# A hybrid attention layer on one core: other K tiles for VectorE's row products, and four kinds of small steps in other places

## The chip, the core and the metric

The kernel runs on one core of a Trainium2 chip. The metric is the device time of one execution in microseconds (us). The core has five engines with an instruction queue each, run in order: TensorE (PE, matrix products; its weight loads are shown as PEld), VectorE (DVE), ScalarE (ACT), GpSimd (POOL) and SyncE (SP), which here issues nearly all loads from main memory. An instruction waits on semaphores for what it needs; while it waits, all behind it on the same engine waits too.

## What is computed

One layer over 256 latent tokens (D = 2048) with a context prefix of 256 tokens, all in float32. Modulation rows come from a conditioning vector and one large matrix (adaLN). The modulated tokens go through one input projection whose columns feed a bidirectional gated linear attention (GLA, 8 heads, with decay factors) and a differential attention (8 heads). Both branches are projected, merged by sigmoid gates, projected again and added to x; then a gated MLP with a width-3 convolution follows. Cut to what matters:

```python
sh1, sc1, g1, sh2, sc2, g2 = split(silu(c) @ w_ada + b_ada, 6)       # w_ada: 2048 x 12288
sh1c, sc1c, ... = split(silu(c_ctx) @ w_ada + b_ada, 6)
h_l, h_c = modulate(rms_norm(x), sh1, sc1), modulate(rms_norm(ctx), sh1c, sc1c)
gq, gk, gv, gr, gaf, gab, dq, dk, dv = split(h @ w_in)               # for h_l and h_c
# GLA, per chunk, forwards and backwards, b = cumsum of log decays:
o_inter = (qc * exp(b)) @ state
o_intra = sum_d qc kc exp(b_i - b_j) @ vc                            # lower triangle
state = exp(b_last) * state + (kc * exp(b_last - b)).T @ vc
o_diff = (softmax(q1 k1) - lam * softmax(q2 k2)) @ v
g_a, g_b = split(sigmoid(h_l @ w_gate + b_gate))
x = x + g1 * (g_a * (ya @ w_proj_gla) + g_b * (yb @ w_proj_diff)) @ w_out
x = x + g2 * (conv_ffn(modulate(rms_norm(x), sh2, sc2)))             # w_up, conv, silu(gate) * val, w_down
```

## The kernel before

**Weights.** Every weight arrives from main memory as 128 x 1024 floats (512 KB) in a buffer "wraw", of which there are four (`fetch`, L231). `split` (L207) makes two halves of it: the upper, whi, is a rounding copy by ScalarE (L212), the lower, wlo, is the difference raw − whi by VectorE (L219). There are three buffers of each. PE then makes three products per piece: upper weight by upper and by lower activation, lower weight by upper activation. A PE wait for wlo means that VectorE came late with that difference.

**First stage** (L384 to about L690). All steps are pinned in program order. For each of the 16 K tiles (128 rows of D) the shift and scale of the modulation are needed before the tile can be swept. For 13 tiles PE computes them: `ada_rows` makes the products "ab" (16 in the code, 32 instructions in the profile) out of four 512 KB quarters of the adaLN matrix ("ada", `load_ada`), then two transposes (L537). They stand inside the sweep of the K tile before. For the three tiles in DOT_TILES, VectorE computes them instead: the matrix lies transposed in "w_ad1t", `load_halves` loads four 512 KB halves of it per tile, and `run_dots` (L426) makes eight row products (a product summed along the row, 128 x 1024) for two streams. The list DOTS says how many of the row products come at each K step, and each half is loaded in the step before its first row product. `dotted` gathers the sums on GpSimd. Then `stage` modulates the tile of each stream (L553, then ScalarE's rounding, L555, then the lower half, L559), and PE sweeps the tile with one piece of `w_in` ("sweep", loaded by `load_sweep`, 448 KB). Loads of the stage go to SP's queue in program order, and "ada" has SLOTS = 10 buffers for quarters and halves together.

**The rest of the adaLN rows.** The other 64 rows of 128 adaLN columns are computed by VectorE alone, as 128 row products "araw" of 128 x 1024 (L379), spread over all later stages to fill VectorE's free time. `ada_load` (L370) loads 512 KB into one of two buffers, `ada_dot` (L377) makes the row product and puts the sum into ada2; it may not come ahead of the last wlo on VectorE (copied[1]). `ada_next(n)` paces both: it adds n to what is due, and each unit due is one product and one load of a later one. With two buffers the load for one product cannot be issued before the product two places ahead of it has ended.

**GLA stage.** The value columns come in chunks (`gv_chunk`, "gvb"), and four pairs of heads (`gla_pair`, L813 on) run beside them under a higher priority. Each pair makes decay sums bfb (cumulative log decays) and rc by scans on VectorE, then rc and qe, exponents by ScalarE times keys and queries by VectorE (L853 and L862), then the scores. The scores are made in groups (RUNS): a whole product, a product of the two chunks (`factors(None)`), and seven levels of the triangle. Each level needs a difference "away" by GpSimd (L930), exponents by ScalarE (L933) and a product e by VectorE (L935). After the first group of scores the decayed keys rc are transposed (`turned_keys`, L867); the states are made with them, and qe is used at the end of the pair.

**Differential stage.** `dv_chunk(0)` (L1051 on) sums four banks over eight pieces of the value weights, each piece split as above, and leaves them to `emptied` (L1054), in which ScalarE copies banks 0 and 2 and VectorE banks 1 and 3 (L1055). Then come query tiles 0 to 3 (`dq_tile`), `dv_chunk(1)`, and the eight heads. `dq_tile` sums one tile of 16 K products from two pieces, adds the two half banks (nraw, L290), squares them and makes head norms with a sum on PE (hss). Each head's attend and scores have a higher priority. Beside the heads run the gate tiles (`gate_tile`, 32 of them, three per head and the rest behind), and query tiles 4 to 7. dv_chunk, dq_tile and gate_tile each call ada_next, gate_tile with an entry of GATE_ADA.

**Tail.** The last stage, "down" (L1419), sums 44 K tiles for each half of the columns. Behind its last pieces come the y steps: `added_rows` (L1428) multiplies a bank by the gate (L1432) and adds the residual row (L1433).

**What sets the order.** Outside the first stage a scheduler places each instruction on its engine's queue by priorities and by its own time estimates, and by the `after` ties written in the code. So instructions may stand in another order than they are written.

Of the kernel before, what the change touches and what calls it, by code (L numbers as in the profile page):

```python
# [13 lines left out]
AF = mybir.ActivationFunctionType  # L14
ALU = mybir.AluOpType
# [3 lines left out]
P = 128  # L19
D = 2048  # L20
T = 256
# [19 lines left out]
UPS = 6  # L41
CONVS = 7
SLOTS = 10
DOT_TILES = 7, 11, 15
DOTS = [0, 0, 2, 2, 2, 2, 1, 2, 2, 3, 1, 2, 2, 3]
LATE_ADA = {13: 1, 14: 2}
ROWS_AT = [4, 3, 2, 1]
WARM = 14
GATE_ADA = [0.25] * 12 + [0.5] * 4 + [0.75] * 8 + [1] * 6 + [0] * 2
NRM = [(0, 0)] * 2 + [(j, j + 1) for j in range(12)] + [(12, 14), (14, 16)]  # L50

_VEC = {}
# [100 lines left out]
def layer_kernel(tc, I, out):  # L153
    nc = tc.nc
    V, S, G, PE = nc.vector, nc.scalar, nc.gpsimd, nc.tensor
    es = ExitStack()
    with es:
# [40 lines left out]
        copied = [None, None]  # L198
# [187 lines left out]
        with tc.tile_pool(name="first", bufs=1) as p1:  # L386
# [21 lines left out]
            cbc = p1.tile([P, D], F32, name="cbc")  # L408
            junk = hp.tile([P, 1024], F32, tag=f"x{KT - 1}", name="junk")
            sums2 = p1.tile([P, len(DOT_TILES), 2, 2, 2], F32, name="sums2")  # L410
            dots = [(0, *d) for d in ((0, 0, 0), (0, 1, 0), (0, 0, 1), (1, 0, 0), (1, 0, 1), (0, 1, 1), (1, 1, 0), (1, 1, 1))]
            dots += [(n, u, q, t) for n in range(1, len(DOT_TILES)) for u in (0, 1) for q in (0, 1) for t in (0, 1)]
            dots_of, at = [], 0
            for n in DOTS + [0] * KT:
                dots_of.append(dots[at:at + n])
# [313 lines left out]
        def ada_next(n):  # L729

            ada_due[0] += n
            while ada_at[0] < min(128, int(ada_due[0])):
                if len(ada_raw) == ada_pool[1]:
                    ada_dot()
                ada_load()
# [16 lines left out]
        with tc.tile_pool(name="gla", bufs=1) as pg:  # L752
# [5 lines left out]
            qk = {}  # L758
# [54 lines left out]
            def gla_pair(p):  # L813
# [35 lines left out]
                        V.tensor_tensor_scan(rc[:, 1, 1:], onec[:, :T - 1], m[:, T:2 * T - 1],  # L849
                                             0.0, op0=ALU.mult, op1=ALU.add)  # L850

                S.activation(rc, rc, AF.Exp, scale=1.0 / 16)
                V.tensor_tensor(rc, rc, qk[p][:, 2:3, :].to_broadcast([P, 2, T]), op=ALU.mult)  # L853
                bl = pg.tile([P, 4], F32, tag="bl", name="bl")
                V.tensor_scalar(bl[:, 0:1], bfb[:, 0, P - 1:P], 1.0 / 16, None, op0=ALU.mult)
                V.tensor_scalar(bl[:, 1:2], bfb[:, 1, P:P + 1], 1.0 / 16, None, op0=ALU.mult)
                qe = pg.tile([P, 2, T], F32, tag="qe", name="qe")
                S.activation(qe[:, 0, :P], bfb[:, 0, :P], AF.Exp, scale=1.0 / 16)
                S.activation(qe[:, 0, P:], bfb[:, 0, P:], AF.Exp, scale=1.0 / 16, bias=bl[:, 0:1])
                S.activation(qe[:, 1, :P], bfb[:, 1, :P], AF.Exp, scale=1.0 / 16, bias=bl[:, 1:2])  # L860
                S.activation(qe[:, 1, P:], bfb[:, 1, P:], AF.Exp, scale=1.0 / 16)
                V.tensor_tensor(qe, qe, qk[p][:, 0:1, :].to_broadcast([P, 2, T]), op=ALU.mult)  # L862

                at = pg.tile([P, 2, 2, T], F32, tag="at", name="at")

# [1 line left out]
                def turned_keys():  # L867

                    b = aux_bank("kT")
                    kn = pg.tile([P, 512], F32, tag="l", name="kn").rearrange("p (a b c) -> p a b c", a=2, b=2)  # L870
                    for d in range(2):
                        for c in range(2):
                            PE.transpose(b[:, (2 * d + c) * P:(2 * d + c + 1) * P], rc[:, d, c * P:(c + 1) * P], ident)
                    return kn, S.copy(kn.rearrange("p a b c -> p (a b c)"), b)
# [42 lines left out]
                def factors(li):  # L917

                    e = pg.tile([P, 2, T], F32, tag="e", bufs=3, name="e")
                    if li is None:  # L920
                        S.activation(e[:, 0, P:], bfb[:, 0, P:], AF.Exp, scale=1.0 / 16)
                        S.activation(e[:, 0, :P], bfb[:, 1, :P], AF.Exp, scale=1.0 / 16)
                        S.activation(e[:, 1, :P], bfb[:, 0, :P], AF.Exp, scale=-1.0 / 16, bias=bl[:, 0:1])
                        S.activation(e[:, 1, P:], bfb[:, 1, P:], AF.Exp, scale=-1.0 / 16, bias=bl[:, 1:2])
                    else:
                        m = LEVELS[li]
                        g = T // (2 * m)
                        away = pg.tile([P, 512], F32, tag="m", name="away")
                        mids = shifted[:, :, m - 1:T:2 * m].unsqueeze(3).to_broadcast([P, 2, g, 2 * m])
                        G.tensor_tensor(away.rearrange("p (a g n) -> p a g n", a=2, g=g),  # L930
                                        bfb.rearrange("p a (g n) -> p a g n", g=g), mids, op=ALU.subtract)
                        for i, (first, step, o, back, sign) in enumerate(((m, T - m, m, -m, 1), (0, T + m, 0, m, -1))):
                            S.activation(view(e[:, i, :], o, [back, 2], [2 * m, g], [1, m]),  # L933
                                         view(away, first, [step, 2], [2 * m, g], [1, m]), AF.Exp, scale=sign / 16)
                    V.tensor_tensor(e, e, qk[p][:, 0:2, :], op=ALU.mult)  # L935
                    return e


# [9 lines left out]
                for n, levels in enumerate(RUNS):  # L948
                    group = ([] if n else whole) + [level(li) for li in levels]
                    if n == 1:  # L950
                        kept = pg.tile([P, 2, T], F32, tag="e", bufs=3, name="e")
                        state = kept[:, 0, :].rearrange("p (a b) -> p a b", a=2)
                        scored(group[::-1], states, [emptied])
                    else:
                        scored(group[::-1])
                    if n == 0:
                        kn, emptied = turned_keys()

                obs = [aux_bank("o", j) for j in range(2)]
# [79 lines left out]
        with tc.tile_pool(name="diff", bufs=1) as pd:  # L1039
# [11 lines left out]
            def dv_chunk(j):  # L1051
                banks = [acc_bank("dvb") for _ in range(4)]

                def emptied(t):  # L1054
                    (V.tensor_copy if t % 2 else S.copy)(dv[:, t, 512 * j:512 * (j + 1)], banks[t])  # L1055


                turn = [6, 7, 0, 1, 2, 3, 4, 5] if j else list(range(8))
                for q in turn:
                    if q in turn[1:3]:  # L1060
                        flush(latest)
                        flush()
                    raw = fetch(I["w_dv"][j, q].rearrange("p a b -> p (a b)"), 1024)
                    both = split(raw, 1024)
                    ws = []
                    for a in range(2):
                        def halves_of(a=a):
                            if j or q > 1:
                                ada_next(0.875 if j else 1)
                            return [w[:, a * 512:(a + 1) * 512] for w in both]  # L1070
                        ws.append((2 * q + a, halves_of))
                    value_rows(banks, ws, 512, 2 * turn[0], 2 * turn[-1] + 1, emptied)
                    if not j and q >= 4:
                        after(V.tensor_tensor(oy[q - 4], oy[q - 4], gr[q - 4], op=ALU.mult), copied[1])
                    if j:
                        nc.gpsimd.dma_start(X4[2 * q][:, 2:, :], A[2 * q + 1])
                        A[2 * q + 1] = X4[2 * q][:, 2:, :]

            def dq_tile(h):
                dq[h] = pd.tile([P, T], F32, tag="dq", bufs=4, name="dq")  # L1080
                b = aux_bank("dq") if h < 2 else acc_bank("dq")
                if h < 2:
                    ada_next(1)
                col_tile(I["w_in"][15 - NGK + h], A, b)
                heads_norm(b, nwt[:, 1:2], lambda o: roped(tp, dq[h], o),
                           *[t[:, h % 2 * T:(h % 2 + 1) * T] for t in nts[:2]], lambda: nts[2][:, h % 2 * T:(h % 2 + 1) * T])
# [90 lines left out]
            for h in range(HEADS):  # L1177
                with tc.high_priority(500):
                    normed_head, emptied = attend(h)
                    if h + 1 < HEADS:  # L1180
                        halves(h + 1)
                        scores(h + 1, emptied)
                    normed_head()
                if h < 4:
                    dq_tile(4 + h)
                for _ in range(3):
                    gate_tile(order.pop(0))
            while order:
# [134 lines left out]
        with tc.tile_pool(name="ffn", bufs=1) as pf:  # L1323
# [101 lines left out]
            def place(at):  # L1425
                return shared(8 + 2 * (at // 2), at % 2, "y")

            def added_rows(h, t, n):  # L1428

                o = slice(1024 * h + 512 * n, 1024 * h + 512 * (n + 1))  # L1430
                y = place(4 * h + 2 * t + n)
                V.tensor_tensor(y, banks[h][t][n], cb[:, o], op=ALU.mult)  # L1432
                V.tensor_tensor(y, y, rows[2 * h + n][t], op=ALU.add)  # L1433
                return y

# [16 lines left out]
                    residual(h, k)  # L1452

            ws = [pieces(k) for k in range(last, FT)]
            y, late = added_rows(1, 1, 1), place(0)
            for n in range(2):
                for t in range(2 - n):
                    for k in range(last, FT):
# [26 lines left out]
```

## Time and profile before

| what | value |
|---|---|
| median of 3 runs | 1657.08 us (1656.51 to 1658.12) |
| the profiled execution | 1658.09 us |
| its span, first to last instruction | 1656.3 us |
| granted TensorE clock | 1.000 |
| ScalarE busy | 904.2 us (55%) |
| GpSimd busy | 289.1 us (17%) |
| bytes moved | 372.75 MB, mean 225 GB/s |
| row products araw, 128 | 161.1 us busy, 1263 ns each |
| wlo by VectorE, 466 | 564.5 us busy, 1212 ns each |

Times in the profile are those of one profiled execution, counted in microseconds from the start of its span, and the rows name an engine, the line of the kernel, the operation and output<-input by the program's names. A timeline row is start, duration, engine, line, operation, shape, number of instructions in the row (x), and in brackets the idle time of the engine just ahead of it and what ended that. "SPq" is a load issued by SP. PE's matmuls overlap a little, so that the step from one start to the next tells more than the durations.

### The profile page before, as it was taken

What the parts mean: (1) busy time and instruction counts of PE and PEld (TensorE: products, weight loads), DVE (VectorE), ACT (ScalarE), POOL (GpSimd) and SP (SyncE); (2) the same over time, 40 slices, a digit from 0 to 9 for tenths busy, and PEclk for the clock granted to TensorE, in tenths of its full rate; (3) what the DMA queues carried; (4) which work ended last, traced back from release to release, by engine and by line L of the source; (5) the groups of instructions that cost most, each with busy time, mean ns of one, the idle gap of its engine ahead of it and who ended that gap; (6) DMA issues with size and microseconds to landing.
All of it is one profiled execution on the core that took longest, in us unless ns stands there. A gap on an engine that the chain in (4) does not pass through costs nothing.

```text
span 1656.3 us, 25739 instructions
## 1 busy us (share of the span) xinstructions
PE 1645.7 (99%) x9509; PEld 1407.3 (85%) x9509; DVE 1303.5 (79%) x2031; ACT 904.2 (55%) x1503; POOL 289.1 (17%) x328
## 2 busy tenths in 40 slices
PE   9999999999999999999999999999999999999998
PEld 7679988888887888888888988888888888888887
DVE  5787888797679888888988887888888888745544
ACT  5235466674346767656645675555555555433332
POOL 0001221230011000001114101122212212684000
PEclk9999999999999999999999999999999999999999
DMA  9996744345785556687887566777777776777764
GB/s 382 408 370 221 237 144 155 117 138 184 248 270 186 176 182 202 228 272 256 265 284 218 181 196 225 233 225 239 241 231 238 225 237 211 210 218 204 221 196 130
DMA packets 111966, 372.75 MB, mean 225 GB/s; under 512 B 14560, under 2 KB 19680, under 8 KB 111840
## 3 DMA queue, kind: packets, MB, share of 16 engines
q1 hardware_dynamic: 102112, 362.51, 66.6%
q0 software_dynamic: 5696, 4.24, 1.0%
q10 hardware_dynamic: 4032, 4.37, 0.8%
q8 instruction: 74, 1.21, 0.3%
q14 instruction: 52, 0.43, 0.1%
HBM read 364.73 MB, written 2.10 MB: 221 GB/s over the span
## 4 chain that ended last, share of the span: by engine, by line
PE 92%; DMA 4%; DVE 3%; issue 1%; ACT 0%; SPq 0%; DVEq 0%
PE down L1419 14%; PE upg L282 9%; PE upv L282 9%; PE gate L282 7%; PE upv L284 5%; PE upg L284 5%; PE sweep L391 4%; PE gate L284 4%; PE mix L282 4%; DMA araw<-in_w_ada 2%; PE mix L284 2%; PE gr L282 2%; PE pga L282 2%; PE pgb L282 2%; PE dk L355 2%; PE dk L356 2%
## 5 line engine op out<-in xcount | busy, mean ns | idle before, releaser
L212 ACT CAST whi<-wraw 128x1024 fp32r<-128x1024 f32 (+3 forms) x502 | 516.1, 1029 | 491.9 <-PE down L1419 138.6
L219 DVE TENSOR_TENSOR wlo<-wraw,whi 128x1024 fp32r<-128x1024 f32 (+3 forms) x466 | 564.5, 1212 | 219.3 <-ACT whi L212 216.8
L282 PE MATMUL upg<-x,whi 128*128 128x512 f32 x656 | 229.0, 391 | 0.0
L282 PE MATMUL upv<-x,whi 128*128 128x512 f32 x656 | 229.0, 391 | 0.0
L1419 PE MATMUL down<-whi,g 128*128 128x512 f32 x698 | 215.0, 389 | 0.0
L284 PE MATMUL upv<-x,wlo 128*128 128x256 f32 x656 | 182.8, 280 | 0.0
L284 PE MATMUL upg<-x,wlo 128*128 128x256 f32 x656 | 182.6, 280 | 0.0
L379 DVE CUSTOM_DVE_ANT_0 araw<-araw,cb 128x1024 f32<-128x1024 f32 x128 | 161.1, 1263 | 24.0 <-DMA araw<-in_w_ada 23.8
L282 PE MATMUL gate<-x,whi 128*128 128x512 f32 x512 | 179.5, 396 | 0.0
L219 POOL TENSOR_TENSOR wlo<-wraw,whi 128x1024 fp32r<-128x1024 f32 x36 | 86.9, 2415 | 395.3 <-ACT whi L212 395.3
L1419 PEld LDWEIGHTS down<-whi,g 128*128 128x128 f32 x698 | 130.9, 188 | 27.2
L282 PEld LDWEIGHTS upg<-x,whi 128*128 128x128 f32 x656 | 122.4, 187 | 26.6
L282 PEld LDWEIGHTS upv<-x,whi 128*128 128x128 f32 x656 | 122.4, 187 | 26.6
L284 PE MATMUL gate<-x,wlo 128*128 128x256 f32 x512 | 139.4, 282 | 0.5 <-DVE wlo L219 0.5
L1419 PE MATMUL down<-wlo,g 128*128 128x512 f32 x349 | 135.9, 389 | 0.8 <-DVE wlo L219 0.8
L1337 DVE SCALAR_TENSOR_TENSOR C<-C,vec 128x255 f32<-128x255 f32 x88 | 105.7, 1202 | 36.6 <-ACT C L1336 36.6
L284 PEld LDWEIGHTS upv<-x,wlo 128*128 128x128 f32 x656 | 123.9, 189 | 0.5
L284 PEld LDWEIGHTS upg<-x,wlo 128*128 128x128 f32 x656 | 123.9, 189 | 0.5
L282 PEld LDWEIGHTS gate<-x,whi 128*128 128x128 f32 x512 | 94.4, 188 | 19.9 <-issue 1.1
L284 PEld LDWEIGHTS gate<-x,wlo 128*128 128x128 f32 x512 | 96.2, 189 | 4.3 <-issue 1.1
L282 PE MATMUL mix<-x,whi 128*128 128x512 f32 x256 | 87.8, 394 | 0.0
L1419 PEld LDWEIGHTS down<-wlo,g 128*128 128x128 f32 x349 | 65.5, 188 | 14.8 <-DVE wlo L219 1.3
(336 smaller groups left out, 3213.9 us busy)
## 6 DMA issues: line engine op xcount, KB each, us to landing
wraw<-in_w_up SPq DMA_DIRECT2D x164, 512.0 KB, 4.6
araw<-in_w_ada SPq DMA_DIRECT2D x128, 512.0 KB, 5.5
wraw<-in_w_down SPq DMA_DIRECT2D x88, 512.0 KB, 4.2
wraw<-in_w_gate SPq DMA_DIRECT2D x64, 512.0 KB, 4.4
wraw<-in_w_in SPq DMA_DIRECT2D x58, 512.0 KB, 4.7
ada<-in_w_ad SPq DMA_DIRECT2D x52, 512.0 KB, 9.9
wraw<-in_w_proj SPq DMA_DIRECT2D x32, 512.0 KB, 4.9
wraw<-in_w_out SPq DMA_DIRECT2D x32, 512.0 KB, 4.8
```

What stands on the lines that cost most here:

```text
L212: copied[0] = S.copy(hi[:, :n], raw)
L219: i = e.tensor_tensor(lo[:, :n], raw, hi[:, :n].bitcast(F32), op=ALU.subtract)
L282: i = PE.matmul(b.rearrange("p (a b) -> p a b", a=2), whi[:, sl], acts[k], start=first, stop=last)
L284: i = PE.matmul(b[:, T:], wlo[:, sl], acts[k][:, 1, :], start=False, stop=last)
L355: matmul(o, whi[:, sl], hi, start=first, stop=False)
L356: matmul(o, whi[:, sl], lo, start=False, stop=False)
L379: i = V.tensor_tensor_reduce(raw, raw, cb[:, q * 1024:(q + 1) * 1024], 1.0, 0.0, op0=ALU.mult, op1=ALU.add, accum_out=ada2[:, j, q:q + 1])
L391: return kept(PE.matmul(*args, **kw))
L1337: V.scalar_tensor_tensor(u[:, 1:], b[:, :T - 1], vcol("conv_w", ct), u[:, 1:], op0=ALU.mult, op1=ALU.add)
L1419: i = PE.matmul(o, g[:, a, ts], w[n][b][:, cols], start=k == first and (a, b) == (1, 0), stop=k == last and b == 1)
```

## The change

Four kinds of change, in the kernel's order:

- DOT_TILES, the K tiles by VectorE in the first stage, are 8, 12 and 15 in place of 7, 11 and 15. DOTS, the row products at each step, follows, and the first tile's row products come in the plain order, both streams of a half together, two products and one half per step at K steps 3 to 6. Before, two halves came at step 2.
- In each GLA pair the exponents and products for rc and qe are put into a function `decayed`, which is called behind the first group of scores and ahead of the turned keys; on VectorE its two products may not come ahead of the last e product made so far (`made[0]`).
- The remaining adaLN rows are paced anew: dv_chunk asks 1.125 in place of 1 a turn in the first chunk and 0.75 in place of 0.875 in the second, dq_tile asks 1 for three query tiles in place of two, the gate tiles ask by another list with the same sum, 17. Query tiles 4 to 7 are made after heads 1, 2, 4 and 5 in place of heads 0, 1, 2 and 3.
- In the tail, the first y product (`added_rows(1, 1, 1)`) is tied behind the last wlo on VectorE.

The number of row products, of matmuls and of bytes stays the same.

```diff
-DOT_TILES = 7, 11, 15
-DOTS = [0, 0, 2, 2, 2, 2, 1, 2, 2, 3, 1, 2, 2, 3]
+DOT_TILES = 8, 12, 15
+DOTS = [0, 0, 0, 2, 2, 2, 2, 1, 2, 2, 3, 2, 3, 3]
-GATE_ADA = [0.25] * 12 + [0.5] * 4 + [0.75] * 8 + [1] * 6 + [0] * 2
+GATE_ADA = [0.25] * 16 + [0.5] * 8 + [1.5] * 6 + [0] * 2
+DQ_AT = {1: 4, 2: 5, 4: 6, 5: 7}
...
-            dots = [(0, *d) for d in ((0, 0, 0), (0, 1, 0), (0, 0, 1), (1, 0, 0), (1, 0, 1), (0, 1, 1), (1, 1, 0), (1, 1, 1))]
-            dots += [(n, u, q, t) for n in range(1, len(DOT_TILES)) for u in (0, 1) for q in (0, 1) for t in (0, 1)]
+            dots = [(n, u, q, t) for n in range(len(DOT_TILES)) for u in (0, 1) for q in (0, 1) for t in (0, 1)]
...
-                S.activation(rc, rc, AF.Exp, scale=1.0 / 16)
-                V.tensor_tensor(rc, rc, qk[p][:, 2:3, :].to_broadcast([P, 2, T]), op=ALU.mult)
...
+                made = []
+                def decayed():
+                    S.activation(rc, rc, AF.Exp, scale=1.0 / 16)
+                    after(V.tensor_tensor(rc, rc, qk[p][:, 2:3, :].to_broadcast([P, 2, T]), op=ALU.mult), made[0])
...
+                    after(V.tensor_tensor(qe, qe, qk[p][:, 0:1, :].to_broadcast([P, 2, T]), op=ALU.mult), made[0])
...
-                    V.tensor_tensor(e, e, qk[p][:, 0:2, :], op=ALU.mult)
+                    made[:] = [V.tensor_tensor(e, e, qk[p][:, 0:2, :], op=ALU.mult)]
...
                     if n == 0:
+                        decayed()
                         kn, emptied = turned_keys()
...
-                                ada_next(0.875 if j else 1)
+                                ada_next(0.75 if j else 1.125)
...
-                if h < 2:
+                if h < 3:
                     ada_next(1)
...
-                if h < 4:
-                    dq_tile(4 + h)
+                if h in DQ_AT:
+                    dq_tile(DQ_AT[h])
...
-            def added_rows(h, t, n):
+            def added_rows(h, t, n, earlier=None):
...
-                V.tensor_tensor(y, banks[h][t][n], cb[:, o], op=ALU.mult)
+                i = V.tensor_tensor(y, banks[h][t][n], cb[:, o], op=ALU.mult)
+                if earlier is not None:
+                    after(i, earlier)
...
-            y, late = added_rows(1, 1, 1), place(0)
+            y, late = added_rows(1, 1, 1, copied[1]), place(0)
```

Lines of the changed kernel lie 1 to 8 further on. What moves on the engines, in three places. First SP's queue in the first stage, from adaLN tile 3 on, before: "ada<-in_w_ad" x4 are the quarters of one tile for PE, "ada<-in_w_ad1t" is a half for VectorE's row products, "wraw<-in_w_sw" a sweep piece.

```order
L363 DMA ada<-in_w_ad 128x1024 x4
L363 DMA ada<-in_w_ad1t 128x1024 x2
L363 DMA wraw<-in_w_sw 128x896
L363 DMA ada<-in_w_ad 128x1024 x4
L363 DMA ada<-in_w_ad1t 128x1024
L363 DMA wraw<-in_w_sw 128x896
L363 DMA ada<-in_w_ad 128x1024 x4
L363 DMA wraw<-in_w_sw 128x896
L363 DMA ada<-in_w_ad 128x1024 x4
L363 DMA ada<-in_w_ad1t 128x1024
```

The same place after the change:

```order
L364 DMA ada<-in_w_ad 128x1024 x4
L364 DMA wraw<-in_w_sw 128x896
L364 DMA ada<-in_w_ad 128x1024 x4
L364 DMA ada<-in_w_ad1t 128x1024
L364 DMA wraw<-in_w_sw 128x896
L364 DMA ada<-in_w_ad 128x1024 x4
L364 DMA ada<-in_w_ad1t 128x1024
L364 DMA wraw<-in_w_sw 128x896
L364 DMA ada<-in_w_ad 128x1024 x4
L364 DMA ada<-in_w_ad1t 128x1024
```

No half stands ahead of tile 4 (the second row of quarters) now and one ahead of tile 5, where two and three stood; the third and the fourth come behind tiles 6 and 7.

Second, VectorE in the first GLA pair, before. "ISA araw" is a row product and the ISA row of 128x1 behind it reads its sum; wlo 128x544 is the lower half of a value piece.

```order
L219 TENSOR_TENSOR wlo<-wraw,whi 128x544
L379 ISA araw,ada_77<-araw,cb 128x1024
L379 ISA ada_77 128x1
L853 TENSOR_TENSOR rc<-rc,qk 128x512
L862 TENSOR_TENSOR qe<-qe,qk 128x512
L935 TENSOR_TENSOR e<-e,qk 128x512 x2
L219 TENSOR_TENSOR wlo<-wraw,whi 128x544
L379 ISA araw,ada_77<-araw,cb 128x1024
L379 ISA ada_77 128x1
L935 TENSOR_TENSOR e<-e,qk 128x512
L219 TENSOR_TENSOR wlo<-wraw,whi 128x544
```

The same place after the change:

```order
L220 TENSOR_TENSOR wlo<-wraw,whi 128x544
L380 ISA araw,ada_77<-araw,cb 128x1024
L380 ISA ada_77 128x1
L940 TENSOR_TENSOR e<-e,qk 128x512 x2
L220 TENSOR_TENSOR wlo<-wraw,whi 128x544
L380 ISA araw,ada_77<-araw,cb 128x1024
L380 ISA ada_77 128x1
L940 TENSOR_TENSOR e<-e,qk 128x512
L862 TENSOR_TENSOR rc<-rc,qk 128x512
L867 TENSOR_TENSOR qe<-qe,qk 128x512
L220 TENSOR_TENSOR wlo<-wraw,whi 128x544
```

The products rc and qe have moved past one wlo, one row product and three e products, and stand ahead of the next wlo.

Third, VectorE at the end of the first dv chunk and the start of the query tiles, before. The first wlo is of query tile 0's first piece, the second of its second, and the two behind the copies of dv are query tile 1's.

```order
L219 TENSOR_TENSOR wlo<-wraw,whi 128x1024
L379 ISA araw,ada_77<-araw,cb 128x1024
L379 ISA ada_77 128x1
L219 TENSOR_TENSOR wlo<-wraw,whi 128x1024
L379 ISA araw,ada_77<-araw,cb 128x1024
L379 ISA ada_77 128x1
L1055 COPY dv<-dvb 128x512 x2
L219 TENSOR_TENSOR wlo<-wraw,whi 128x1024 x2
L290 TENSOR_TENSOR nraw<-dq,nraw 128x256
```

The same place after the change:

```order
L220 TENSOR_TENSOR wlo<-wraw,whi 128x1024
L380 ISA araw,ada_77<-araw,cb 128x1024
L380 ISA ada_77 128x1
L380 ISA araw,ada_77<-araw,cb 128x1024
L380 ISA ada_77 128x1
L220 TENSOR_TENSOR wlo<-wraw,whi 128x1024
L380 ISA araw,ada_77<-araw,cb 128x1024
L380 ISA ada_77 128x1
L380 ISA araw,ada_77<-araw,cb 128x1024
L380 ISA ada_77 128x1
L1061 COPY dv<-dvb 128x512 x2
L220 TENSOR_TENSOR wlo<-wraw,whi 128x1024 x2
```

Between the first wlo and the copies stand four row products in place of two; one of them comes ahead of the second wlo in addition, and two in place of one between it and the copies. Behind the last two wlo, one more row product follows ahead of nraw.

## What the change does to the time: the prediction

> **What bounds the kernel now.** I read the page first: the span, then the busy shares. Columns of the second row: busy us, share of the span, instructions.
>
> ```profile
> span 1656.3 us, 25739 instructions
> PE 1645.7 (99%) x9509; PEld 1407.3 (85%) x9509; DVE 1303.5 (79%) x2031; ACT 904.2 (55%) x1503; POOL 289.1 (17%) x328
> ```
>
> TensorE (PE) is the bound: it lacks 10.6 us of the span, and the change takes no matmul out. All that it can win or lose is time in which PE stands still. So the second view is PE's waits (line waited on: total us, times, longest).
>
> ```profile
> PE down L1419 <- DVE wlo L219: 0.8, 1, 0.8
> PE ab L391 <- DMA ada<-in_w_ad: 0.8, 2, 0.6
> PE gvb L295 <- DVE wlo L219: 0.8, 1, 0.8
> PE gate L284 <- DVE wlo L219: 0.5, 1, 0.5
> PE dvb L293 <- DVE nraw L290: 0.3, 1, 0.3
> ```
>
> Each part of the change touches one of these five. They add up to 3.2 us; the time from issue to issue gives a little more, and I use that below. The profiled execution took 1658.09 us, 1.8 outside its span and 1.0 above the median of 1657.08; I sum against the profiled one and take the 1.0 off at the end. About 0.2%, 3.3 us, can be told from no change.
>
> **Part 1: other K tiles by VectorE in the first stage.** PE's timeline, an adaLN tile (ab, 32 matmuls) each time and the sweep matmul behind it, and the one row of the window table (last number GB/s):
>
> ```profile
> 40.60 1.93 PE L391 MATMUL ab<-ada,ccol_s 128*32 128x256 f32 x32
> 42.46 0.50 PE L391 MATMUL sweep<-whi,x 128*128 128x512 f32 x1
> 47.28 1.80 PE L391 MATMUL ab<-ada,ccol_s 128*32 128x256 f32 x24
> 49.72 0.64 PE L391 MATMUL ab<-ada,ccol_s 128*32 128x256 f32 x8 [0.64 <-DMA ada<-in_w_ad]
> 50.29 0.50 PE L391 MATMUL sweep<-whi,x 128*128 128x512 f32 x1
> 55.54 1.50 PE L391 MATMUL ab<-ada,ccol_s 128*32 128x256 f32 x24
> 57.81 0.50 PE L391 MATMUL sweep<-whi,x 128*128 128x512 f32 x1
> 69.33 0.39 PE L391 MATMUL sweep<-whi,x 128*128 128x512 f32 x1
> 40.00:50.00 10.00, 9.27 (x87) 5.27 (x86) 7.97 (x15) 2.23 (x5) 0.00 (x0) 1.00 1.03 407
> ```
>
> An unhindered tile takes 42.46 − 40.60 = 1.86. Tile 4 takes 3.01 (1.15 too many), tile 5 takes 2.27 (0.41). The queue is full, 407 GB/s: 512 KB take 1.29 us, 448 KB of sweep 1.13. Before tile 4 the old order loads two 512 KB halves more, and before tile 5 as well (one comes ahead of it rather than three). So the last quarter of tile 4, here at 49.72, lands 2.6 earlier, near 47.1, and PE asks for it near 48.7 (47.28 and three quarters of 1.86). Tile 5 lands near 54.6 and is asked for near 55.8 (55.54 + 1.4 − 1.15); both stalls go, 1.56. From there a tile's loads (one half, one sweep, four quarters: 1.29 + 1.13 + 5.16 = 7.6) are longer than its PE time (57.81 − 50.29 − 0.41 = 7.1), so the margin shrinks by some 0.5 a tile: tile 6 still has 0.7, tile 7, new on PE, 0.25. The next thing late is VectorE at tile 7:
>
> ```profile
> 64.76 1.23 DVE L429 CUSTOM_DVE_ANT_0 junk<-ada,cb 128x1024 f32<-128x1024 f32 x1 [1.03 <-DMA ada<-in_w_ad1t]
> 67.71 0.89 DVE L553 SCALAR_TENSOR_TENSOR x<-x,shsc,z 128x256 f32<-128x256 f32 x2
> ```
>
> The first tile's fourth half is now loaded behind tile 7's quarters and lands near 71.0. Its two row products stand ahead of tile 7's first modulation: 67.71 − 64.76 = 2.95 later, at 73.95, and the first hi about 1.0 after that, 74.95. PE wants it at 69.33 − 1.56 + 7.1 = 74.9. I take 0.2 as the new wait. **Part 1: −1.4**, bounds −1.6 and −0.5 (if loads land 0.5 later than I sum).
>
> **Part 2: the decayed factors behind the first scores.** VectorE in the first GLA pair, PE's late matmul and GpSimd:
>
> ```profile
> 172.99 1.54 DVE L853 TENSOR_TENSOR rc<-rc,qk 128x512 f32<-128x512 f32 x1
> 174.45 0.68 DVE L862 TENSOR_TENSOR qe<-qe,qk 128x512 f32<-128x512 f32 x1
> 175.05 2.17 DVE L935 TENSOR_TENSOR e<-e,qk 128x512 f32<-128x512 f32 x2
> 177.14 0.71 DVE L219 TENSOR_TENSOR wlo<-wraw,whi 128x544 fp32r<-128x544 f32 x1
> 177.91 0.39 PE L295 MATMUL gvb<-wlo,x 128*128 128x272 f32 x1 [0.78 <-DVE wlo L219]
> 174.88 1.19 POOL L930 TENSOR_TENSOR away<-bfb 128x512 f32<-128x512 f32 x1 [0.90 <-ACT e L933]
> ```
>
> The products rc and qe, 1.54 + 0.68 = 2.2 us, leave the place ahead of wlo at 177.14. wlo then starts near 175, or near 176.7 if the e products now meet GpSimd's subtraction. The stall was about 0.9 between issues. **−0.9**, bounds −0.95 and −0.3. At their new place the products are covered by the first scores, which PE runs between that weight tile and the next; without the cover they cost what rival 2 says.
>
> **Part 3: adaLN row products at other weights, last query tiles elsewhere.** At two places a product leaves the front of something PE waits for:
>
> ```profile
> 469.31 1.23 DVE L379 CUSTOM_DVE_ANT_0 araw<-araw,cb 128x1024 f32<-128x1024 f32 x1 [3.50 <-DMA araw<-in_w_ada]
> 519.73 1.21 DVE L379 CUSTOM_DVE_ANT_0 araw<-araw,cb 128x1024 f32<-128x1024 f32 x1
> 522.61 1.21 DVE L219 TENSOR_TENSOR wlo<-wraw,whi 128x1024 fp32r<-128x1024 f32 x1
> ```
>
> In the second dv chunk four products instead of five stand ahead of nraw of query tile 3; the fifth waited 3.50 us for its load. PE's stall there goes: **−0.5** (bounds −0.5, 0). In the gate stage the product of 519.73 is gone, 1.2 us, so wlo of 522.61 is in time: **−0.65** (−0.67 to −0.4). The moved query tiles only change which matmuls lie beside which head, and the late gates get two products a tile at most, 2.4 us of VectorE behind a whole tile's matmuls: I cost both at nothing; a gate tile without that cover would lose up to those 2.4.
>
> But two products are added where the queue was tight, the end of the first dv chunk. VectorE, SP's queue, PE's first use (from the chain), and the loads of that stretch from issue to landing:
>
> ```profile
> 432.35 1.23 DVE L379 CUSTOM_DVE_ANT_0 araw<-araw,cb 128x1024 f32<-128x1024 f32 x1 [1.92 <-DMA araw<-in_w_ada]
> 433.50 1.22 DVE L219 TENSOR_TENSOR wlo<-wraw,whi 128x1024 fp32r<-128x1024 f32 x1
> 435.35 1.23 DVE L379 CUSTOM_DVE_ANT_0 araw<-araw,cb 128x1024 f32<-128x1024 f32 x1 [0.63 <-DMA araw<-in_w_ada]
> 436.50 1.28 DVE L1055 COPY dv<-dvb 128x512 f32<-128x512 f32 x2
> 437.70 1.22 DVE L219 TENSOR_TENSOR wlo<-wraw,whi 128x1024 fp32r<-128x1024 f32 x1
> 436.61 0.33 SPq L373 DMA_DIRECT2D araw<-in_w_ada  x1
> 440.84 0.47 PE dq L282 x2
> DMA to landing us min/median/max: 3.6/5.2/6.6
> ```
>
> Now: dot, wlo, dot, two copies, then wlo of query tile 1 (437.70 to 438.92), 2 us before PE wants it, near 441.1 (two matmuls with the upper half come first). After: both dots, wlo, two more dots, copies, that wlo. There are two buffers, so the load for the last of these dots can be issued only when the dot of 435.35 has ended, as at 436.61 here. It lands 5.2 later, 441.8 (between 440.2 and 443.2). Then the dot 1.15, the copies 1.2 and wlo 1.22 follow in VectorE's order: 3.57 more, 445.4. PE waits 445.4 − 441.1 = 4.3 at the median landing, 2.7 at the fastest and 5.7 at the slowest. **I take +4.0**, between the fastest and the median and nearer to the median; bounds +2.7 and +5.7. Behind that wlo on VectorE are the second wlo, a dot and nraw of query tile 0; its sums are wanted at 449 plus the wait, so nothing more is late. On SP's queue the weight fetches behind the two added loads go out some 3 to 6 us later, with whole tiles in hand.
>
> [...]
>
> **Part 4: the first y product behind the last wlo.**
>
> ```profile
> 1642.66 1.05 ACT L212 CAST whi<-wraw 128x1024 fp32r<-128x1024 f32 x1 [1.67 <-PE down L1419]
> 1642.89 0.69 DVE L1432 TENSOR_TENSOR y<-down,cb 128x512 f32<-128x512 f32 x1 [0.64 <-PE down L1419]
> 1644.22 1.22 DVE L219 TENSOR_TENSOR wlo<-wraw,whi 128x1024 fp32r<-128x1024 f32 x1
> ```
>
> The y steps end at 1644.22; whi is ready at 1643.75. So wlo starts 0.47 sooner and no more, as ACT's cast bounds it: **−0.5** (−0.5 to −0.3). The y product loses nothing: it is used only after PE's last 128-row product.
>
> **Sum:** −1.4 − 0.9 − 0.5 − 0.65 − 0.5 + 4.0 = +0.05, so 1658.1 profiled and **1657.1** as the median. The ends of the gains add up to −4.2 and −1.5; with the wait at its bounds that is 1655.6 to 1661.3. As all ends hardly meet, I take 1655.6 to 1660 as the likeliest case's own range.
>
> **The rivals.** *1. No wait at query tile 1* (the loads there come early enough, or PE gets there later for a reason I don't see): the gains stay, 1657.1 − 4.0 = 1653.1. For it: wlo is 2 us early now. Against: the dot of 435.35 itself waited 0.63 for its load, and one of 3.6 us would still leave 2.7. Chance 0.18.
>
> *2. Slower: the moved products meet GpSimd at the scores.* The place is the last score level of each pair:
>
> ```profile
> 188.34 0.68 DVE L935 TENSOR_TENSOR e<-e,qk 128x512 f32<-128x512 f32 x1
> 189.32 1.54 PE sc L899 x24
> ```
>
> e ends at 189.02, 0.3 before PE's scores. A product of this size took 1.54 where GpSimd ran and 0.68 where it didn't; if one more in each pair is caught, e is later by 0.86, 0.3 of which has cover in this pair. At the full price in four pairs that is 3.4: 1660.5. It decides once the delay exceeds 0.3. Against it: the new place, at the first scores, lies some 10 us ahead of that level (177.91 to 188.34). Chance 0.12. [...]
>
> *3. The loads of the first stage don't move up* (something else holds the queue, tile 7 missing its 0.25): 1.4 is not won, 1658.5. For it: the margin. Against: a queue at 407 GB/s is ordered by what is ahead. Chance 0.07.
>
> **How the numbers follow.** My forecast has 0.63, the rivals 0.18, 0.12 and 0.07. Faster by over 3.3 us (under 1653.8): most of rival 1 (0.16) and a thin end of the forecast (0.02), 0.18. Slower by over 3.3 us (above 1660.4): more than half of rival 2 (0.08) and the forecast's upper end (0.04), 0.12. Within: 0.70. The range leaves nearly half of rival 1 below (0.08) and those 0.12 above: 1653.0 to 1660.4.
>
> **What would show it.** In the profile after: the two waits of ab on DMA gone, wlo before gvb gone from PE's waits, dvb on nraw, gate on wlo and down on wlo gone or under 0.5; a new row, dq on wlo, of about 4 us near 439. If that row is missing or under 1, I am wrong and rival 1 is right; if sc waits for e in each pair, rival 2; if ab still waits for DMA, rival 3.

## The result: slower by 8.3 us, and where the time went

The changed kernel takes 1665.29 us (median of 6 runs, 1664.65 to 1666.54) where the kernel before takes 1657.01 (6 runs beside them, 1656.30 to 1658.12): a ratio of 1.0050, 95% interval 1.0038 to 1.0063. The forecast was 1657.1 with 1653.0 to 1660.4, so it was wrong. The profiled execution took 1665.19; its page begins:

```profile
span 1663.4 us, 25735 instructions
PE 1648.0 (99%) x9509; PEld 1408.8 (85%) x9509; DVE 1299.5 (78%) x2031; ACT 905.1 (54%) x1503; POOL 288.3 (17%) x328
```

PE now lacks 15.4 us of the span instead of 10.6. Its own busy time has grown by 2.3 us with the same 9509 matmuls, so they have also become slower somewhere. PE's waits after the change (total, times, longest):

```profile
PE dq L285 <- DVE wlo L220: 3.4, 1, 3.4
PE upg L283 <- DVE x L1300: 1.7, 1, 1.7
PE pT L1142 <- DVE pe L1139: 1.6, 1, 1.6
PE gate L285 <- DVE wlo L220: 1.3, 2, 0.7
...
PE sweep L392 <- ACT x L555: 1.0, 3, 0.4
...
PE down L1425 <- DVE wlo L220: 0.4, 1, 0.4
```

Of the five waits that the change aims at, ab, gvb and dvb are gone from this profile, down is halved, and the gate wait of 523 us is gone too (the two here lie at 719 and 731 us). The wait of dq on wlo is the one that was forecast. But upg is new, the gate waits are new, pT is longer. Comparing where the same matmul starts in the two profiles, the changed kernel is 1.5 us ahead at K tile 8 of the first stage, 0.6 ahead at its end, 1.8 ahead at the first query tile, 3.4 behind after the second, 5.6 behind at the end of the gates, 7.5 behind in the up stage, and 7.1 at the end. The two profiled executions lie 7.1 us apart, the medians 8.3: the one of before was 1.1 slower than its median.

**The dq wait.** VectorE between the two query tiles:

```profile
432.77 1.23 DVE L380 CUSTOM_DVE_ANT_0 araw<-araw,cb 128x1024 f32<-128x1024 f32 x1 [2.10 <-DMA araw<-in_w_ada]
...
435.59 1.23 DVE L380 CUSTOM_DVE_ANT_0 araw<-araw,cb 128x1024 f32<-128x1024 f32 x1 [0.44 <-DMA araw<-in_w_ada]
...
439.31 1.23 DVE L380 CUSTOM_DVE_ANT_0 araw<-araw,cb 128x1024 f32<-128x1024 f32 x1 [2.49 <-DMA araw<-in_w_ada]
...
440.46 1.28 DVE L1061 COPY dv<-dvb 128x512 f32<-128x512 f32 x2
441.66 2.35 DVE L220 TENSOR_TENSOR wlo<-wraw,whi 128x1024 fp32r<-128x1024 f32 x2
```

Row products that each wait for their load, then the copies, then the wlo that PE needs; from the last product's start to the end of that wlo it is 3.6 us, as worked out. The load of that last product:

```profile
434.03 0.33 SPq L374 DMA_DIRECT2D araw<-in_w_ada  x1
```

It was issued when the product two places ahead (432.77) had ended, 2.6 us earlier than the 436.61 of the prediction, and landed 5.1 later, as predicted. The prediction had kept the first two of the four products at their old times, 432.35 and 435.35; they ran at 429.43 and 432.77. PE, ahead by then, asked for the wlo at 439.4, 1.7 earlier than the 441.1 of the prediction. The two errors nearly cancel. What was not worked out stands in the next view: PE by window, with its granted clock (the number behind the busy time) behind the wait.

```profile
440.00:443.00 3.00, 0.07 (x1) 1.00 0.60 208
443.00:444.00 1.00, 1.00 (x6) 0.98 0.51 135
444.00:445.00 1.00, 1.00 (x5) 0.50 0.66 184
445.00:446.00 1.00, 1.00 (x5) 0.50 0.83 303
446.00:447.00 1.00, 1.00 (x5) 0.50 0.93 287
447.00:448.00 1.00, 1.00 (x6) 0.82 0.80 193
```

About 1 us after PE has started again its clock is halved for over 3 us: 0.02 + 3 x 0.50 + 0.18 = 1.7 us of work lost, on top of the wait.

**The late gate and the up stage.** On VectorE, two row products stand before one gate weight, the second waiting for its load (first three rows), and one stray product stands among the last modulated tiles of the up stage (last row):

```profile
714.47 1.22 DVE L380 CUSTOM_DVE_ANT_0 araw<-araw,cb 128x1024 f32<-128x1024 f32 x1
...
717.26 1.23 DVE L380 CUSTOM_DVE_ANT_0 araw<-araw,cb 128x1024 f32<-128x1024 f32 x1 [0.96 <-DMA araw<-in_w_ada]
...
718.41 1.22 DVE L220 TENSOR_TENSOR wlo<-wraw,whi 128x1024 fp32r<-128x1024 f32 x1
...
957.24 1.22 DVE L380 CUSTOM_DVE_ANT_0 araw<-araw,cb 128x1024 f32<-128x1024 f32 x1
```

Behind the stray product, on PE, the wait for the last modulated tile:

```profile
969.01 0.50 PE L283 MATMUL upg<-x,whi 128*128 128x512 f32 x1 [1.72 <-DVE x L1300]
```

### The profile page after: what moved, and what is told of

Read it like the earlier page. It is cut to its first block, busy times and chain, and to the rows that moved or that the text cites. A ratio compares the mean times of both kernels' runs of the same rounds, so it can differ in the third digit from the quotient of the medians.

```text
span 1663.4 us, 25735 instructions
## 1 busy us (share of the span) xinstructions
PE 1648.0 (99%) x9509; PEld 1408.8 (85%) x9509; DVE 1299.5 (78%) x2031; ACT 905.1 (54%) x1503; POOL 288.3 (17%) x328
## 4 chain that ended last, share of the span: by engine, by line
PE 88%; DMA 7%; DVE 3%; issue 1%; ACT 1%; SPq 0%; DVEq 0%; ACTq 0%
PE down L1425 14%; PE upv L283 9%; PE upg L283 9%; PE gate L283 6%; PE upv L285 5%; PE upg L285 5%; DMA araw<-in_w_ada 4%; PE mix L283 4%; PE gate L285 3%; PE sweep L392 2%; PE mix L285 2%; PE pga L283 2%; PE pgb L283 2%; PE gr L283 2%; PE dq L283 2%; PE dk L357 2%
```

## The experiments

Theory A: each late place is an effect of its own of the new paces, and the other three parts give small gains. Theory C: one late place takes VectorE's lead and the others follow from it. Each run is compared with the kernel before, run on the same chip in turn with it (its median there was 1656.73 to 1656.78).

**The paces and query tiles as before; the other three parts stay.**

```diff
-GATE_ADA = [0.25] * 16 + [0.5] * 8 + [1.5] * 6 + [0] * 2
-DQ_AT = {1: 4, 2: 5, 4: 6, 5: 7}
+GATE_ADA = [0.25] * 12 + [0.5] * 4 + [0.75] * 8 + [1] * 6 + [0] * 2
+DQ_AT = {0: 4, 1: 5, 2: 6, 3: 7}
...
-ada_next(0.75 if j else 1.125)
+ada_next(0.875 if j else 1)
...
-if h < 3:
+if h < 2:
```

> The changed kernel with all adaLN paces and the places of query tiles 4 to 7 as before; the other three parts stay. Theory A (the loss is in the paces alone, at several places of its own, the other parts give what the trace of the changed kernel shows: -1.5 by K tile 8, +0.9 back by K tile 12, -1.2 in the GLA stage, -0.5 in the tail): 1657.0 - 2.3 = 1654.7 us, no wait of dq, upg or late gates for VectorE. Theory B (the other parts cost something that only shows later, for instance by the moved products): about 1657 or above.

Measured 1655.53, ratio 0.9994 (0.9985 to 1.0003): 1.2 less than before, not clear of no change. No dq, upg or late gate wait is left. So the loss lies in the paces, and the gain of the rest is about half of what theory A took from the one profile.

**The paces and query tiles alone, on the kernel before.** The same edit the other way round.

> The kernel before with the new paces and places of query tiles alone. Theory A: all of the loss and none of the other gains: 1665.3 + 2.3 = 1667.6 us, with the waits dq <- wlo 3.5, pT 1.6, gate <- wlo 1.3 in two, upg <- x 1.7, and the granted clock at 0.5 for some 4 us behind the dq wait. Theory B: under 1665.

Measured 1666.28, ratio 1.0060 (1.0047 to 1.0074): 9.6 us lost by this part alone, a little less than theory A's 1667.6. The pT wait is 0.5 us here as in the kernel before, not 1.6, and the late gates wait 0.7 in the list of waits, not 1.3; the half clock lasts 6.8 us, twice as long. Its longest wait of PE:

```profile
PE dq L285 <- DVE wlo L220: 3.8, 1, 3.8
```

Windows behind it, PE's granted clock again behind the busy time (it is 0.50 from 443 us on):

```profile
444.00:445.00 1.00, 1.00 (x4) 0.50 0.57 131
...
448.00:449.00 1.00, 1.00 (x4) 0.50 1.05 229
449.00:450.00 1.00, 1.00 (x5) 0.59 0.73 233
```

And VectorE in the GLA stage, whose code is that of the kernel before:

```profile
175.67 0.71 DVE L220 TENSOR_TENSOR wlo<-wraw,whi 128x544 fp32r<-128x544 f32 x1
```

The same wlo, behind the same rc and qe products, starts at 175.67 here and at 177.14 in the profile of before, and PE doesn't wait for it: gvb is not among this run's waits. The profiles of three more kernels below with this GLA code (the first stage alone, and both idle reductions) have no gvb wait either. The gvb stall of 0.9 us belonged to the one profiled execution of the kernel before, not to the kernel.

**Half a product less.**

```diff
-                ada_next(13 / (KT - 2))
+                ada_next(12.5 / (KT - 2))
```

> The changed kernel with the merge stage asking 12.5 adaLN products in place of 13, so that the running sum is again what it was before from the mix stage on; no product is added or left out. Theory A, phase: the changed paces ask 0.5 more in sum, so one product more is loaded before the up stage, and the flush at the end of that stage puts it on VectorE ahead of the last modulated tiles; without it upg <- x (1.7 in the waits, 1.9 from issue to issue) goes: 1663.4 us. Rival theory C (upg waits because VectorE has lost its lead at the earlier waits): unchanged, 1665.3.

Measured 1662.89, ratio 1.0036 (1.0023 to 1.0048): 2.4 less than the changed kernel, and the upg row is gone from PE's waits while dq (3.8) stays. That is theory A's phase: the new paces ask 13.5 + 12 + 3 + 17 products where the old ones asked 12 + 14 + 2 + 17, half a product more. The sum is cut to whole products; from the mix stage on one more has been loaded, and the flush of the buffers at the end of the up stage has to make it just there. Theory C is out for this wait.

**The first chunk's pace back to 1.**

```diff
-                                ada_next(0.75 if j else 1.125)
+                                ada_next(0.75 if j else 1)
...
-                ada_next(13 / (KT - 2))
+                ada_next(14.5 / (KT - 2))
```

> The changed kernel with 1 in place of 1.125 products a turn in the first dv chunk; the 1.5 products are asked in the merge stage instead, so the running sum is as in the changed kernel from there on. Theory A: the dq wait goes with its slow clock (3.5 + 1.7 = 5.2), pT, late gates and upg stay: 1660.1 us. Rival theory C (the first wait takes VectorE's lead and the rest follow from it): pT, gates and upg go too, 5.2 + 1.1 + 1.6 + 1.9 less, 1655.5.

Measured 1658.56, ratio 1.0012 (1.0003 to 1.0021): 6.7 less than the changed kernel, between the two theories. The dq wait and the half clock are gone; so are pT and the late gates, and two others have come (the first is theory A's, the next two are new):

```profile
PE upg L283 <- DVE x L1300: 1.7, 1, 1.7
...
PE pga L283 <- DVE ya L239: 0.8, 1, 0.8
PE hss L665 <- DVE nlo L239: 0.8, 1, 0.8
```

So the dq wait is due to 1.125, and part of the later waits hangs on the lead that is lost there.

**An idle reduction in place of the products.** Does the wait halve the clock, or do the changed loads? The kernel before, with one VectorE instruction of a chosen length, at a high priority, ahead of that wlo:

```diff
+i = (V.tensor_copy if t % 2 else S.copy)(dv[:, t, 512 * j:512 * (j + 1)], banks[t])
+if not j and t == 3:
...
+    after(V.tensor_reduce(dv[:, 0, 512:514], cb[:, :2048].unsqueeze(1).to_broadcast([P, 2, 2048]), axis=AX.X, op=ALU.max), i)
```

> The kernel before with one idle reduction on VectorE (4096 elements a row, an estimate of 4.9 us from 1.2 ns an element in the rows of TENSOR_REDUCE) between the copies at the end of the first dv chunk and wlo of query tile 1; its result is not used, no pace and no load is changed. Theory D (a PE gap of a certain length by itself halves the granted clock for some us behind it): PE waits about 2.7 us at dq; if the length at which it starts lies between 2.7 and 3.5, clock 1.0 and + 2.7 = 1659.5; if it lies below, clock 0.5 and + 4.4 = 1661.2. Rival E (the half clock comes from something else in the changed paces, such as the loads): clock 1.0, 1659.5.

It took 4.41 us. PE's start behind the wait:

```profile
441.79 0.38 PE L284 MATMUL dq<-x,wlo 128*128 128x256 f32 x1 [1.90 <-DVE wlo L219]
```

Two windows there:

```profile
442.00:443.00 1.00, 1.00 (x7) 1.00 0.28 29
443.00:444.00 1.00, 1.00 (x8) 1.00 0.78 246
```

And its longest wait:

```profile
PE pT L1139 <- DVE pe L1136: 2.2, 2, 1.3
```

From issue to issue PE stands 2.1 us, less than the 2.7 expected, and the clock stays at 1.00 there. Yet the run takes 1662.55, ratio 1.0033 (1.0020 to 1.0045), 5.8 more than before and more than either theory had: pT waits 2.2 in place of 0.5, and the waits of oss and gate behind it grow too. The profiled execution is the fastest of the five, 1660.74; what the others lost on top of it is not shown. So here a late dq, with the old paces, made the first heads late again: theory C, for these. It doesn't always do so: with the paces alone PE waited longer at dq (3.75 us idle ahead of that matmul, 1.90 here), and pT stayed at 0.5.

The longer one (`[P, 3, 1664]`, and the slice 512:515):

> As the run with the short reduction, with 4992 elements a row, an estimate of 6.0 us: PE waits about 3.8 us. Theory D: the granted clock is 0.5 for some 4 us behind the wait, + 3.8 + 1.7 = 1662.3. Rival E: clock 1.0 throughout, + 3.8 = 1660.6.

It took 5.34 us. PE's two starts:

```profile
441.03 0.49 PE L282 MATMUL dq<-x,whi 128*128 128x512 f32 x1 [1.23 <-ACT whi L212]
443.44 0.54 PE L284 MATMUL dq<-x,wlo 128*128 128x256 f32 x1 [1.92 <-DVE wlo L219]
```

The windows behind them:

```profile
443.00:444.00 1.00, 0.56 (x2) 0.76 0.00 0
444.00:445.00 1.00, 1.00 (x4) 0.50 0.40 82
445.00:446.00 1.00, 1.00 (x5) 0.50 0.94 299
446.00:447.00 1.00, 1.00 (x5) 0.53 0.85 328
447.00:448.00 1.00, 1.00 (x7) 1.00 0.75 274
```

Here PE stands 1.4 and 2.2 us with one matmul between, and the clock goes to 0.50 for 3.4 us (0.48 + 2 + 0.94 of the windows). This execution took 1663.56. The other four have a mean granted clock of 1.000 against 0.999 in this one, so there the clock was not halved for that long. The median of the five, 1662.50, ratio 1.0034 (1.0021 to 1.0046), lies near theory D's 1662.3 by luck: it is no more than in the run with the short reduction. What the profile shows is that neither the new paces nor their loads are needed for the half clock: in this execution idle PE time was enough (theory D). An unbroken wait did it in all five profiles with 3.5 us or more (3.5 to 4.3 from issue to issue), and 2.1 us did not.

**The late gates evenly.**

```diff
-GATE_ADA = [0.25] * 16 + [0.5] * 8 + [1.5] * 6 + [0] * 2
+GATE_ADA = [0.25] * 16 + [0.5] * 8 + [1.125] * 8
```

> The changed kernel with [1.125] * 8 in place of [1.5] * 6 + [0] * 2 at the end of the gate list (same sum). Theory A: the two waits of late gates for wlo (0.8 and 0.9 from issue to issue) come from two products before one weight tile and go: 1665.3 - 1.6 = 1663.7, unless the products that now come at the last two gates delay the merge. Rival theory C (VectorE has no lead left there): the waits stay, 1665.3.

Measured 1663.28, ratio 1.0040 (1.0027 to 1.0054): 2.0 less than the changed kernel. No gate row is left in its waits, and dq (3.3) and upg (1.7) stay. Without two products before one weight the late gates don't wait.

**Query tiles 4 to 7 after heads 0 to 3 again.**

```diff
-DQ_AT = {1: 4, 2: 5, 4: 6, 5: 7}
+DQ_AT = {0: 4, 1: 5, 2: 6, 3: 7}
```

> The changed kernel with query tiles 4 to 7 after heads 0 to 3 again. Theory A: the places of the query tiles cost nothing, the dq wait, pT, the late gates and upg stay: 1665.3 within 0.7. Rival H (the query tiles cover the first heads, and moving them makes the pT wait longer by 1.1): 1664.2 or less.

Measured 1663.24, ratio 1.0042 (1.0029 to 1.0054): 2.1 less, though one of its five runs (1665.33) reaches into those of the changed kernel; by the medians not theory A. The head of its waits:

```profile
PE dq L285 <- DVE wlo L220: 4.2, 1, 4.2
PE upg L283 <- DVE x L1300: 1.7, 1, 1.7
```

Both the pT row and the gate rows are gone, with the list of late gates unchanged: in this profile the second product of a pair still waits for its load (1.38 and 1.20 us), but the wlo behind it is in time:

```profile
715.95 1.22 DVE L220 TENSOR_TENSOR wlo<-wraw,whi 128x1024 fp32r<-128x1024 f32 x1
```

It starts 2.5 us earlier than its like in the changed kernel (718.41), while PE comes to that weight only 1.1 earlier. So in these profiles the late gates need both, two products and the moved query tiles. Whether pT is due to the move I leave open, since it differs between kernels that do not differ there (below).

**Evener row products for K tile 12**, on the run with the paces back.

```diff
-DOTS = [0, 0, 0, 2, 2, 2, 2, 1, 2, 2, 3, 2, 3, 3]
+DOTS = [0, 0, 0, 2, 2, 2, 2, 2, 2, 2, 2, 2, 3, 3]
```

> The run with the paces back, with one row product of K tile 12 made at step 7 rather than at step 10 (two at each of the steps 7 to 10). Theory A: the late modulation of K tile 11 (three products ahead of it, 0.9 us lost) goes: 1655.5 - 0.9 = 1654.6. Rival F (the loads of the halves, not the products, make it late, and one half loaded a step earlier delays the quarters of K tile 9): no gain or a loss up to 1.3, 1655.5 to 1656.8.

Measured 1655.47, ratio 0.9994 (0.9985 to 1.0002): no gain over 1655.53, so theory A is out. In its trace K tile 12 is 0.3 us earlier, a third of what was to come back, and the first scores and pT wait that much and more longer.

**The first stage alone, on the kernel before.**

> The kernel before with the first stage of the changed kernel alone (K tiles 8, 12 and 15 by VectorE). Theory A: the two waits of ab on DMA go (1.3), 0.25 comes back at K tile 7 and some 0.6 to 0.9 by K tile 12: -0.4, 1656.4. Rival: as forecast, -1.4, 1655.4.

Measured 1656.41, ratio 0.9998 (0.9989 to 1.0006): 0.4 less, as theory A has it, though an interval that holds 1 shows no gain. The ab wait on DMA is gone from its waits. Where the gain goes again, in the trace of the changed kernel: PE is still 1.5 us ahead when it comes to K tile 13, and waits there for the modulated tile, which VectorE makes behind three row products.

```profile
113.13 0.50 PE L392 MATMUL sweep<-whi,x 128*128 128x512 f32 x1 [0.23 <-ACT x L555]
```

**Parts 2 and 4 alone: decayed factors and the tied y product.**

> The kernel before with the decayed factors behind the first scores and the tied y product alone. Theory G (the gvb stall of 0.9 in the profile of before belongs to that one execution, since the run with the paces alone has the same GLA code and no such stall): only the 0.5 of the tail is won, 1656.3. Rival (the stall is in every execution): -0.9 - 0.5, 1655.3.

Measured 1656.27, ratio 0.9996 (0.9988 to 1.0005): 0.5 less, theory G, though this interval holds 1 too. Two of its waits:

```profile
PE pT L1143 <- DVE pe L1140: 1.2, 1, 1.2
...
PE ab L392 <- DMA ada<-in_w_ad: 0.8, 2, 0.6
```

The paces and heads are those of the kernel before here, whose pT wait was 0.5 in its profile; from issue to issue this gap is 1.4 here, 0.65 before, 0.6 in the run with the first stage alone, and 1.7 in the changed kernel. It lies behind two row products that wait for their loads, and differs by up to 0.8 us between kernels that have the same code and the same paces there.

The dvb wait is not among this run's waits, nor among those of the run with the paces back and of the one for K tile 12, which have the old pace of that chunk too. Yet a row product still stands just ahead of nraw of query tile 3 here:

```profile
467.42 1.23 DVE L380 CUSTOM_DVE_ANT_0 araw<-araw,cb 128x1024 f32<-128x1024 f32 x1 [2.50 <-DMA araw<-in_w_ada]
```

It waits for its load 2.50 us here and 3.50 in the profile of the kernel before. With the first stage alone (3.69) dvb still waits 0.2. So the dvb stall, too, depends on when that load lands, and its going is not shown to come from the new paces. The gate wait near 521 us is different: it is in every profile with the old start of the gate list (with the idle reductions 2 to 5 us later) and in none with the new one.

**One product less in the second dv chunk**, on the run with the paces back.

```diff
-ada_next(0.875 if j else 1)
+ada_next(0.8125 if j else 1)
...
-GATE_ADA = [0.25] * 12 + [0.5] * 4 + [0.75] * 8 + [1] * 6 + [0] * 2
+GATE_ADA = [0.25] * 12 + [0.5] * 4 + [0.75] * 8 + [1] * 6 + [0.5] * 2
```

> The run with the paces back, and 0.8125 in place of 0.875 a turn in the second dv chunk, with the one product asked at the last two gate tiles instead. Theory A: the product ahead of the late gate weight (0.67 at 520 us) goes, no new wait: 1655.5 - 0.65 = 1654.9, clear of the kernel before. Rival theory C (VectorE is behind there whatever is taken out): no gain, 1655.5.

Measured 1655.96, ratio 0.9996 (0.9986 to 1.0005): no gain. The edit missed its aim: the row product ahead of that gate weight is still there and the stall is 0.69 us; the one that left stood somewhere else. It decides nothing. No version here is clearly faster than the kernel before.

## Why the prediction was wrong, step by step

- **Part 1, −1.4: the step was right to K tile 7 and stopped too early.** Both ab waits went (the changed kernel was 1.5 ahead at K tile 8, with 0.25 at tile 7 where I had put 0.2). But I followed the new lists only as far as the first new tile. Three row products now stand ahead of the modulation of K tile 11 and three ahead of that of K tile 13. Up to there the changed kernel is still 1.5 ahead; 0.6 goes at tile 13 and 0.3 more by tile 15. Net 0.4 in the run that has this part alone.
- **Part 2, −0.9: the mechanism moved as said and won nothing.** The stall was in one execution and I took it for the kernel's. There was a sign of it in what I had quoted: the profiled execution took 1.0 us more than the median, and I carried that 1.0 as a constant instead of asking which stalls it was.
- **Part 3, the places that were to gain: right for the gate, not shown for dvb.** The gate of 523 us behaved as forecast. The dvb row is gone as well, but three runs with the old pace of that chunk (the paces back, K tile 12, parts 2 and 4 alone) don't have it either, so its −0.5 was read from one execution, as gvb's −0.9 was.
- **Part 3, the dq wait, +4.0: right in mechanism, and in size partly by luck** (3.6 from issue to issue, 3.5 to 4.3 in five profiles with that pace). The two buffers, the load and VectorE's order behind it are as forecast; but the deciding load went out 2.6 earlier than I summed and PE came 1.7 earlier, and the two nearly cancel. What failed in the sum is "PE waits 4.3 at the median landing": I priced a long PE stall at its own length. It costs 1.7 us more in the changed kernel, as the clock halves behind it, and about 3 in the run with the paces alone (PE worked at half clock through the five windows from 444 us on and most of the sixth). The profiles show a clock of 1.00 behind 2.1 us of idle PE (the short reduction) and of 0.50 behind each of the five unbroken waits of 3.5 to 4.3 us, for 3.4 us in the changed kernel and 6.8 in the run with the paces alone; where between 2.1 and 3.5 us of wait it starts, no run shows. Behind 1.4 + 2.2 us (the long reduction) it fell in the one execution that was profiled, and the mean clock of the other four, 1.000, leaves no room for it.
- **Part 3, "I cost both at nothing": wrong for both.** The late gates waited 1.6 us together, and in the profiles without the double products, without the moved query tiles or without the late dq they didn't. I had named the cover, a whole tile's matmuls, but not put the second product's load (0.96 and 1.46 us of waiting) and VectorE's own other work between the two products into it.
- **Not in the prediction at all: upg, +1.9.** The paces were read as rates and never summed. With 0.5 product more in sum, one product appears some 500 us later, at a place that no line of the change touches.
- **Part 4, −0.5: right.** The stall went from 1.01 to 0.54 us in the profiles; by the medians 0.5 can't be told from no change.
- **The rivals:** none was the case. A slower case by a product caught at the scores did not occur: sc is not among PE's waits in the profile, and rc and qe took 0.68 us each at their new place in all four pairs. The case that did, several waits from one list of paces, was not among them.

In sum: −0.4 (first stage) − 0.5 (dvb) − 0.65 (gate) − 0.5 (tail) + 3.6 + 1.7 (dq and clock) + 1.6 (late gates) + 1.9 (upg) = 6.75, of 8.3 measured. Without dvb, which the runs don't credit to the change, it is 7.25, and the rest, 1.05, is as much as pT grew between the two profiles (0.65 to 1.7). That is not pinned to a cause, since pT differs by as much as 0.8 between kernels alike there. Settled are upg (the phase of the sum) and the dq wait with its half clock. For the late gates the runs show that a late dq, the double products and the moved query tiles each have a part, and don't divide it; what makes pT longer stays open.

## What to carry to other kernels

Where a list of rates paces work, add it up: compare the running sum of before and after at every place where it is cut to whole numbers or flushed, since half a unit moves an instruction hundreds of microseconds away. A stall that one profile shows is worth its length only if other executions have it; where the profiled time is above the median, look for the stall that makes it so before selling its removal. And a long wait of PE can cost more than its length: here every profiled wait of 3.5 us or more at one place was followed by a half clock, which cost another 1.7 us or more.

## What the runs showed of the hardware

- An idle PE of 2.1 us left the granted clock at 1.00 (the short reduction). A wait of 3.5 to 4.3 us was followed by a clock of 0.50 in all five profiles that have one, for 3.4 us in the changed kernel and 6.8 in the run with the paces alone, at a cost of 1.7 to 3 us. The fall came about 1 us after PE had resumed in the one, and 0.7 us before in the other.
- Two waits of 1.4 and 2.2 us with a single matmul between (the long reduction) were followed by a clock of 0.50 for 3.4 us in the profiled execution; in the other four of that run the mean clock, 1.000, leaves no room for it.
- In the GLA stage, with the same code up to there, VectorE's queue was 1.5 us later in one execution than in another (wlo at 177.14 before and at 175.67 with the paces alone), and PE stalled 0.9 us in the one and not in the other.
